# Memory attention of a hybrid decoder layer: score sums with the sequence pair innermost, the last head's queries spread by products, a score step moved ahead of the sums, the weights in two tiles

## The chip, the cores and the metric

The kernel runs on one core of a Trainium2 chip. The metric is the device time of one execution in microseconds (us): 939.5 before the change, the median of three runs (939.25, 939.5 and 940.07). A core has five engines with a queue of instructions each, which run side by side and wait for one another by semaphores: PE (TensorE, matrix products into PSUM; its weight loads are listed as PEld), DVE (VectorE), ACT (ScalarE), POOL (GpSimd) and SP (SyncE, which issues the DMAs here). Within one queue instructions start in the order in which they were built.

## The reference, cut to what matters

One layer of a decoder serves a prompt group (512 rows) and a sample group (8 sequences of 4 new rows) with the same weights: a mixer of mLSTM and differential attention, a cross-attention into 256 memory tokens, and a gated MLP with a short convolution. The change lies in the cross-attention alone:

```python
def mem_attend(h, mk, mv, w_mq, w_mo):
    B, T, _ = h.shape
    q = (h @ w_mq).reshape(B, T, MEM_HEADS, MEM_HEAD_DIM)
    s = jnp.einsum('bqhd,bkhd->bhqk', q.astype(jnp.float32), mk.astype(jnp.float32)) * (MEM_HEAD_DIM ** -0.5)
    p = jax.nn.softmax(s, axis=-1)
    o = jnp.einsum('bhqk,bkhd->bqhd', p, mv.astype(jnp.float32)).reshape(B, T, D_MODEL)
    return o.astype(h.dtype) @ w_mo
```

There are 4 heads of 256 dimensions. The prompt attends to keys and values computed from its own memory tokens (mk, mv); each sample sequence has its own cached K and V (`cache_mem_k`, `cache_mem_v`, 256 x 1024 values each).

## The kernel before, in words

All matrices are f32. For precision the large products take a value as a rounded "hi" part and the remainder as a "lo" part: `split` (L146, L147) has ACT cast the hi part and DVE subtract it. The products of the queries, `hqT` by `w_mq`, run in eight column blocks (L485); their evacuation `ev_q` leaves the prompt's queries as `qh` and `ql` and the 32 sample rows as `qs`.

**Prompt.** Eight steps, one for each head and half of the rows, pass through three stages: `ch_soft` (scores `sca`, 12 products, then maximum `cnm`, exponential and division into `cp`), `ch_turn` (four transposes `cpt` on PE, split into `pT`), and `ch_out` (for a whole head, 12 products `cpo`, split into `oT`). `pipe` issues them so that in turn t come the out of step t - 3, the turn of step t - 2 and the scores of step t; each `next(prompt)` issues one turn. The turns are the fill between the sample group's parts.

**Sample.** For 8 sequences x 4 rows x 4 heads, products are 32 columns wide, and four of them lie side by side in PE's 128 columns, one column group each. `mq_spread` copies each head's 32 sample queries to `qx` (heads 0 and 1) or `both` (heads 2 and 3), four groups of 32 partitions and four positions each, 16 small copies for each of heads 2 and 3, 32 for the others; zeros around them were set ahead. `mk_load` loads K images of two halves, `mk_turn` has DVE transpose them in blocks of 32. `mk_scores` (L1519) computes the scores `ssc` of a pair of sequences, first with heads 0 and 1 (e = 0), then with heads 2 and 3 (e = 1), and ACT copies them to `sc` (L1522). `mk_sum` (L1536) adds up the four column groups of the eight scores with 16 products `pS` against a selector, into one bank: sequence pair i goes to the 32 columns from 32 i. Then `mem_softmax`, which is scheduled with high priority: maximum from `pS` (L1553), `over_groups` (two block transposes, a reduction and a copy, L1540 to L1545), subtraction (L1554), exponential on ACT (L1555), sum, division (L1556, L1557), transposes `spt` on PE (L1566), and ACT's copies (L1569) to the weights `caz`, 128 x 2048, cleared by POOL (L1559). `mv_out` (L1587) multiplies them with the V images into `pso`. After the last head's `cpo`, the projection with `w_mo` begins (L411 to L413).

**What sets the order.** The code is written in the order shown; a scheduler places each instruction on its engine's queue by its readiness, with `burst` and `issue_after` holding a group of products together. Buffers come from pools: `S` (11 large tiles), `N` (5), `stage()` (6), and PSUM pools for `mmp` (5 banks) and `at` (3). A tile takes the slot of the pool's least recently used one, so which tile is asked for decides when a later load, such as `cr` (the 24 small loads of the convolution's state and weights, L1646 to L1648, in an N tile), finds room.

## Time and profile before

| | us |
|---|---|
| median of 3 runs | 939.5 |
| the profiled execution, on its own | 939.88 |
| its span, from the first to the last instruction | 938.1 |
| PE busy | 914.0 (97%) |
| DVE, ACT, POOL busy | 607.4 (65%), 377.8 (40%), 223.7 (24%) |
| mean granted TensorE clock | 0.996 |
| cross-attention, from the queries to the first product with w_mo | about 395 to 479 |

The table is of the one execution that the profiler took. A row of the timeline gives start, duration, engine, line, operation, output and inputs, a count, and in brackets how long the engine had been idle and what released it. Rows overlap a little, since the ends of pipelined instructions are modelled; where a cost is taken from rows, the distance from one start to the next counts. A product of plain f32 values is two PE instructions in the trace.

### The profile page before, as it was taken

How to read it: one execution, taken by the hardware profiler on the slowest of the kernel's cores; microseconds unless marked ns; L12 is line 12 of the kernel's file. 1: busy time of each engine (PE TensorE's matmuls, PEld its weight loads, DVE VectorE, ACT ScalarE, POOL GpSimd, SP SyncE). 2: the span in 40 equal slices, each digit the busy share in tenths (PEclk: the TensorE clock that was granted, in tenths of full speed). 3: DMA queues.
4: the chain of work that ended last, by engine and by line, in shares of the span. 5: the costliest groups of instructions: out<-in, count | busy, mean ns of one | idle time of the engine just before them, and what ended most of it. 6: DMA issues, size and time to landing. Idle time of an engine off the chain costs nothing.

```text
span 938.1 us, 17455 instructions
## 1 busy us (share of the span) xinstructions
PE 914.0 (97%) x6778; PEld 798.0 (85%) x6778; DVE 607.4 (65%) x1130; ACT 377.8 (40%) x728; POOL 223.7 (24%) x474
## 2 busy tenths in 40 slices
PE   7999999999999999999999999999999999999994
PEld 5899787879866778998777899889988998999974
DVE  5845144565887438686645778637757775776767
ACT  5745233344586447724434533322212222222232
POOL 6611000034442116570000553001100110110114
PEclk9999999999999999999999999999999999999998
DMA  8950023334780339967956632062054304413023
GB/s 286 311 180 11 1 90 138 90 103 161 243 296 8 136 117 298 310 201 243 312 189 172 198 115 69 26 180 69 27 135 135 92 5 120 128 48 90 24 94 117
DMA packets 120834, 130.59 MB, mean 139 GB/s; under 512 B 8599, under 2 KB 86264, under 8 KB 120752
## 3 DMA queue, kind: packets, MB, share of 16 engines
q1 hardware_dynamic: 114568, 125.96, 42.8%
q10 hardware_dynamic: 6184, 3.53, 1.3%
q8 instruction: 53, 0.87, 0.4%
q14 instruction: 29, 0.24, 0.1%
HBM read 112.54 MB, written 16.93 MB: 138 GB/s over the span
## 4 chain that ended last, share of the span: by engine, by line
PE 79%; DVE 8%; DMA 5%; ACT 3%; issue 3%; POOL 2%; SPq 0%; DVEq 0%; ACTq 0%; POOLq 0%
PE mm L485 31%; PE mm L411 6%; PE mm L412 6%; PE mm L413 6%; PE mm L472 4%; PE mm L1837 3%; PE mm L1841 3%; PE mm L1840 3%; PE sda L1256 2%; DVE xb L1165 2%; DMA wst<-in_cache_mem_k_dram 1%; PE mm L390 1%; PE cpo L1480 1%; DVE wslot L147 1%; PE oda L1284 1%
## 5 line engine op out<-in xcount | busy, mean ns | idle before, releaser
L485 PE MATMUL mm<-fT,wslot 128*128 128x256 f32 x1872 | 235.9, 288 | 0.0
L485 PEld LDWEIGHTS mm<-fT,wslot 128*128 128x128 f32 x1872 | 234.3, 188 | 1.8 <-issue 0.8
L146 ACT CAST wslot<-wst 128x1024 fp32r<-128x1024 f32 x125 | 130.7, 1050 | 261.0 <-issue 72.5
L147 DVE TENSOR_TENSOR wslot<-wst,wslot 128x1024 fp32r<-128x1024 f32 x125 | 154.3, 1238 | 81.7 <-ACT wslot L146 81.1
L1837 PE MATMUL mm<-wslot,act 128*128 128x512 f32 (+1 forms) x180 | 69.3, 387 | 0.0
L1840 PE MATMUL mm<-wslot,act 128*128 128x512 f32 (+1 forms) x172 | 67.0, 391 | 0.0
L1841 PE MATMUL mm<-wslot,act 128*128 128x512 f32 (+1 forms) x172 | 66.8, 392 | 0.0
L1739 POOL COPY cvo<-u 128x2 f32<-128x2 f32 x43 | 10.4, 243 | 217.1 <-DVE u L1737 217.1
L411 PE MATMUL mm<-wslot,hT 128*128 128x512 f32 x128 | 51.3, 402 | 0.0
L413 PE MATMUL mm<-wslot,hT 128*128 128x512 f32 x128 | 51.0, 399 | 0.0
L485 PE MATMUL mm<-hT,wslot 128*128 128x256 f32 (+1 forms) x384 | 50.9, 289 | 0.0
L412 PE MATMUL mm<-wslot,hT 128*128 128x512 f32 x128 | 50.8, 397 | 0.0
L1734 DVE TENSOR_TENSOR u<-mm,rsb 128x256 f32<-128x256 f32 x43 | 18.1, 423 | 48.9 <-PE mm L485 48.8
L485 PEld LDWEIGHTS mm<-hT,wslot 128*128 128x128 f32 x384 | 49.2, 188 | 0.5 <-issue 0.2
L1837 PEld LDWEIGHTS mm<-wslot,act 128*128 128x128 f32 x180 | 34.3, 191 | 8.0 <-issue 0.4
L1841 PEld LDWEIGHTS mm<-wslot,act 128*128 128x128 f32 x172 | 32.3, 188 | 6.9 <-issue 0.4
L1840 PEld LDWEIGHTS mm<-wslot,act 128*128 128x128 f32 x172 | 32.3, 188 | 6.9
L1751 ACT ACTIVATE c<-c 128x560 f32<-128x560 f32 x21 | 14.1, 672 | 56.8 <-DVE c L1745 56.7
L1745 DVE SCALAR_TENSOR_TENSOR c<-u,cvT,c 128x560 f32<-128x560 f32 x43 | 34.3, 798 | 0.9
L1744 DVE SCALAR_TENSOR_TENSOR c<-u,cvT,c 128x560 f32<-128x560 f32 x43 | 34.1, 793 | 0.2
L1852 DVE TENSOR_TENSOR yp<-mm,yp 128x512 f32<-128x512 f32 (+1 forms) x41 | 27.1, 672 | 5.1 <-PE mm L1841 5.1
L413 PEld LDWEIGHTS mm<-wslot,hT 128*128 128x128 f32 x128 | 24.1, 188 | 5.0
(493 smaller groups left out, 1858.0 us busy)
## 6 DMA issues: line engine op xcount, KB each, us to landing
wst<-in_w_up_dram SPq DMA_DIRECT2D x42, 512.0 KB
wst<-in_w_in_dram SPq DMA_DIRECT2D x28, 512.0 KB
wst<-in_w_down_dram SPq DMA_DIRECT2D x20, 512.0 KB
kvt<-in_cache_mem_k_dram SPq DMA_DIRECT2D x10, 512.0 KB
kvt<-in_cache_mem_v_dram SPq DMA_DIRECT2D x10, 512.0 KB
wst<-in_w_mk_dram SPq DMA_DIRECT2D x8, 512.0 KB
xb<-in_x_prompt_dram SPq DMA_DIRECT2D x8, 512.0 KB
wst<-in_cache_dk_dram SPq DMA_DIRECT2D x16, 256.0 KB
```

Of the source, the lines that this page charges most:

```text
L146: nc.scalar.copy(out=hi, in_=src)
L147: (eng or nc.vector).tensor_tensor(out=lo, in0=src, in1=f32(hi), op=SUB)
L411: mm(ps[b], lhsT=xt.hi(k, c0, c0 + n), rhs=s[:, 0, kk, :], start=(k == 0), stop=False)
L412: mm(ps[b], lhsT=xt.hi(k, c0, c0 + n), rhs=s[:, 1, kk, :], start=False, stop=False)
L413: return mm(ps[b], lhsT=xt.lo(k, c0, c0 + n), rhs=s[:, 0, kk, :], start=False, stop=(k == nk - 1))
L472: done[0] = mm(ps, lhsT=s[:, l, k, :], rhs=x(k, c0, c1), start=(k == 0 and l == 0 and x == xt.hi), stop=(k == 7 and x == xt.lo))
L485: mm(ps[i], lhsT=s[:, l, k, :], rhs=x(k, c0, c1), start=(k == 0 and j == 0), stop=(k == 7 and j == 2))
L1744: STT(out=c, in0=u[:, 1:EXT - 1], scalar=w[1], in1=c, op0=MUL, op1=ADD)
L1745: STT(out=c, in0=u[:, 0:EXT - 2], scalar=w[0], in1=c, op0=MUL, op1=ADD)
L1837: mm(ps, lhsT=t[:, 0, c0:c0 + P], rhs=s[:, 0, i % 2, cs], start=st, stop=False)
L1840: mm(ps, lhsT=t[:, 0, c0:c0 + P], rhs=s[:, 1, i % 2, cs], start=False, stop=False)
L1841: return mm(ps, lhsT=t[:, 1, c0:c0 + P], rhs=s[:, 0, i % 2, cs], start=False, stop=en)
```

## The change

1. **Queries of the last head.** The 16 copies of head 3 are replaced: four products against `four` (four copies of the identity's slices, made once by POOL) spread `qs` to all four partition groups in PSUM (`qsp`), and four copies, two on DVE and two on ACT, bring them to `both`. `qh` is evacuated ahead of the spread.
2. **Sums.** `mk_sum` runs over the sequence pair i innermost, so successive products go to different column groups; before, i was outermost and four in a row went to one.
3. **A score step ahead.** `pipe` is replaced by `steps`. At t = 6 it issues the scores of step 6 first and yields, which lets them be issued ahead of `mk_sum`; out and turn follow in the next call.
4. **Weights in two tiles.** `caz` is two N tiles of 128 x 1024, cleared after the fifth sequence's scores, instead of one S tile of 128 x 2048.

```diff
+    four = T2([P, 4, P], "four")
+    nc.gpsimd.tensor_copy(out=four.rearrange("p j (g m) -> p j g m", g=4), in_=view(ident, 0, [(NS, 4), (0, 4), (1, NS)]))
 
     def mq_spread(h):
 
+        if h == 3:
+            ps = at("qsp")[:, :256].rearrange("p (c j r) -> p c j r", c=2, j=4)
+            for j in range(4):
+                mm(ps[:, :, j], lhsT=four[:, j], rhs=qs[:, 6:8], start=True, stop=True)
+            for g in range(4):
+                o = slice(NS * g, NS * g + NS)
+                copy = nc.scalar.copy if g % 2 else VCP
+                copy(out=both[o, :, :, :, 1, g, :].rearrange("p c j n t -> p c (j n) t"),
+                     in_=ps[o].rearrange("p c j (n t) -> p c (j n) t", t=TS))
+            return
         for g in range(4):
-            copy = nc.scalar.copy if h == 3 and g > 1 else nc.gpsimd.tensor_copy
+            copy = nc.gpsimd.tensor_copy
...
                 nc.scalar.mul(out=qs[:, m, :], in_=ps[:, n:n + NS], mul=1.0 / 16.0)
-                if m % 2 == 1:
+                if m % 2 == 1 and m < 7:
                     mq_spread(m // 2)
             nc.scalar.mul(out=q, in_=ps[:, :n], mul=1.0 / 16.0)
+            if i == 1 and m == 7:
+                mq_spread(3)
...
-        for i in range(NB // 2):
-            for h in range(2):
-                for e in range(2):
+        for h in range(2):
+            for e in range(2):
+                for i in range(NB // 2):
...
-        az = S([P, 2, H, NB * NS], F32, "caz")
-        nc.gpsimd.memset(az, 0.0)
...
-            nc.scalar.copy(out=view(az, c * 1024, [(256, H), (36, NB), (1, TS)]),
+            nc.scalar.copy(out=view(az[c], 0, [(256, H), (36, NB), (1, TS)]),
...
-    prompt = pipe(8, ch_soft, lambda i: None, ch_turn, ch_out)
+    def steps():
+        for t in range(11):
+            soft, rest = step(t)
+            if t == 6:
+                soft()
+                yield
+                rest()
+            else:
+                rest()
+                soft()
+            yield
+
+    prompt = steps()
...
+        if b == 4:
+            for _ in range(2):
+                az.append(N("caz").rearrange("p (h n) -> p h n", h=H))
+                nc.gpsimd.memset(az[-1], 0.0)
+    next(prompt)
     mk_sum(t)
     with tc.high_priority():
-        az = mem_softmax()
+        mem_softmax()
```

`step(t)` returns two functions: `soft` calls `ch_soft(t)`, `rest` calls `ch_out(t - 3)` and `ch_turn(t - 2)`.

How the built order differs at three places. On PE, where the last queries meet the first score pair; before, from the first products of pair (0,1) on:

```order
L1519 MATMUL ssc<-wst,qx 32x2x32 x34
L1468 MATMUL cpt<-cpk,cp 128x128 x4
L1519 MATMUL ssc<-wst,qx 32x2x32 x30
L1450 MATMUL sca<-mkT,qh 128x256 x2
L1450 MATMUL sca<-mkT,ql 128x256
```

and after:

```order
L1533 MATMUL ssc<-wst,qx 32x2x32 x16
L1415 MATMUL qsp<-qs,four 128x2x32 x4
L1533 MATMUL ssc<-wst,qx 32x2x32 x16
L1482 MATMUL cpt<-cpk,cp 128x128 x4
L1464 MATMUL sca<-mkT,qh 128x256 x2
L1464 MATMUL sca<-mkT,ql 128x256
```

The spreading products stand between the two sequences' first halves, and the scores of step 3 (sca) now come ahead of the pair's second half, the 32 products with `both`. On DVE the copies of that spread, in the changed kernel:

```order
L1467 TENSOR_REDUCE cnm<-sca 128x2
L1516 STREAM_TRANSPOSE kvt<-kvt 128x1024
L147 TENSOR_TENSOR pT<-cpt,pT 128x256
L1419 COPY qx<-qsp 32x64x4
L1516 STREAM_TRANSPOSE kvt<-kvt 128x1024
L1471 RECIPROCAL csu<-csu 128x2
L147 TENSOR_TENSOR pT<-cpt,pT 128x256
L1419 COPY qx<-qsp 32x64x4
```

The two transposes are those of K image 7. The second place is that of the sums. On PE, before:

```order
L1519 MATMUL ssc<-kvt,qx 32x128 x32
L1536 MATMUL pS<-sc,cpk 32x2x64 x12
L1480 MATMUL cpo<-pT,mvN 128x512 x2
L1536 MATMUL pS<-sc,cpk 32x2x64
L1480 MATMUL cpo<-pT,mvN 128x512 x5
L1536 MATMUL pS<-sc,cpk 32x2x64 x3
L1480 MATMUL cpo<-pT,mvN 128x512 x5
L1468 MATMUL cpt<-cpk,cp 128x128 x4
```

and after, where the 12 sca products of step 6, of which the last two rows are shown, stand between the scores and the sums:

```order
L1464 MATMUL sca<-mkT,qh 128x256 x2
L1464 MATMUL sca<-mkT,ql 128x256
L1550 MATMUL pS<-sc,cpk 32x2x64 x3
L1494 MATMUL cpo<-pT,mvN 128x512 x2
L1550 MATMUL pS<-sc,cpk 32x2x64 x13
L1494 MATMUL cpo<-pT,mvN 128x512 x10
L1482 MATMUL cpt<-cpk,cp 128x128 x8
```

On DVE behind the sums, before (oT is the lo part of out(3), one for each `cpo`):

```order
L1459 TENSOR_SCALAR cp<-cp,csu 128x256 x2
L1553 TENSOR_REDUCE spc<-pS 128x4
L147 TENSOR_TENSOR oT_5337<-cpo,oT_5336 128x512
L1540 STREAM_TRANSPOSE spc<-spc 128x32
L1541 TENSOR_REDUCE spc<-spc 128x8
L1544 COPY spc<-spc 128x32
L1545 STREAM_TRANSPOSE spc<-spc 128x32
L147 TENSOR_TENSOR oT_5337<-cpo,oT_5336 128x512
L1554 TENSOR_TENSOR spc<-pS,spc 128x256
```

and after:

```order
L1473 TENSOR_SCALAR cp<-cp,csu 128x256 x2
L147 TENSOR_TENSOR oT_5332<-cpo,oT_5331 128x512 x2
L1567 TENSOR_REDUCE spc<-pS 128x4
L147 TENSOR_TENSOR pT<-cpt,pT 128x256 x2
L1554 STREAM_TRANSPOSE spc<-spc 128x32
L1467 TENSOR_REDUCE cnm<-sca 128x2
L147 TENSOR_TENSOR pT<-cpt,pT 128x256
L1555 TENSOR_REDUCE spc<-spc 128x8
L147 TENSOR_TENSOR pT<-cpt,pT 128x256
L1558 COPY spc<-spc 128x32
L1559 STREAM_TRANSPOSE spc<-spc 128x32
```

Both lo parts stand ahead of the maximum now. The third place is SP's queue of DMAs. Before, the `cr` loads stand between K and V images:

```order
L1498 DMA kvt<-in_cache_mem_k_dram 128x1024 x8
L1646 DMA cr<-in_state_conv_dram 16x896
L1647 DMA cr<-in_w_dw_dram 3x896
L1648 DMA cr<-in_b_dw_dram 1x896
L1646 DMA cr<-in_state_conv_dram 16x896
L1647 DMA cr<-in_w_dw_dram 3x896
L1648 DMA cr<-in_b_dw_dram 1x896
L1498 DMA kvt<-in_cache_mem_k_dram 128x1024 x2
```

and after they stand behind nearly all V images:

```order
L1512 DMA wst<-in_cache_mem_k_dram 128x1024 x6
L1512 DMA kvt<-in_cache_mem_k_dram 128x1024 x10
L1588 DMA wst<-in_cache_mem_v_dram 128x1024 x6
L1588 DMA kvt<-in_cache_mem_v_dram 128x1024 x8
L1689 DMA cr<-in_state_conv_dram 16x896
L1690 DMA cr<-in_w_dw_dram 3x896
```

More of the change, by code (lines that the diff above doesn't have):

```diff
@@ L1568, in mem_softmax @@
         for c in range(2):
-            nc.scalar.copy(out=view(az, c * 1024, [(256, H), (36, NB), (1, TS)]),
+            nc.scalar.copy(out=view(az[c], 0, [(256, H), (36, NB), (1, TS)]),
                            in_=pT[:, c * P:c * P + P].rearrange("p (h b t) -> p h b t", h=H, b=NB))
-        return [az[:, 0], az[:, 1]]
     def mv_load(b):
@@ L1588, in mv_out, with step, soft, rest @@
                            rhs=vts[b][c][:, 256 * h:256 * h + 256], start=((b, c) == VORD[0]), stop=((b, c) == VORD[-1])).ins
-    prompt = pipe(8, ch_soft, lambda i: None, ch_turn, ch_out)
+    az = []
+    def step(t):
+        def soft():
+            if t < 8:
+                ch_soft(t)
+        def rest():
+            if 0 <= t - 3 < 8:
+                ch_out(t - 3)
+            if 0 <= t - 2 < 8:
+                ch_turn(t - 2)
+        return soft, rest
+    def steps():
[10 more added lines that the diff above has]
+    prompt = steps()
     pS = at("pS")[:, :256]
```

## The prediction

> **What bounds the kernel now.** I read the page first, then the stretches, PE's waits, and PE's timeline in the stretch that the diff touches.
>
> ```profile
> PE 79%; DVE 8%; DMA 5%; ACT 3%; issue 3%; POOL 2%; SPq 0%; DVEq 0%; ACTq 0%; POOLq 0%
> 430.00:480.00 50.00, 46.46 (x745) 37.38 (x744) 32.61 (x73) 25.17 (x76) 3.78 (x10) 1.00 0.89 305
> 480.00:545.00 65.00, 65.00 (x400) 53.23 (x399) 41.39 (x73) 29.03 (x58) 17.57 (x28) 1.00 0.58 167
> 545.00:900.00 355.00, 354.69 (x2538) 331.45 (x2541) 248.29 (x431) 94.80 (x114) 46.32 (x190) 1.00 0.28 79
> ```
>
> The chain that ended last is PE for 79%. The rows below it are stretches: length, busy time of PE, PEld, DVE, ACT, POOL, then granted clock, DMA share, GB/s. From 480 to 900 us PE never rests, at full clock: what the change does before 479, where the output projection starts, arrives at the end of the kernel undiminished. In 430 to 480 PE idles 3.54 us of 50, and PE's waits name where:
>
> ```profile
> PE ssc L1519 <- DVE ql L1434: 1.5, 1, 1.5
> PE pso L1587 <- ACT caz L1569: 1.0, 1, 1.0
> PE spt L1566 <- DVE spc L1557: 0.8, 1, 0.8
> ```
>
> So nearly everything here costs PE time; the sum is: where does PE stand at the start of the first L411 product, now 479.04. I walk the built order of the changed kernel with durations from these rows, in three stretches, against the profiled execution's 939.88 us.
>
> **First stretch, queries and the first score pairs.** Columns: start, duration, engine, line, operation.
>
> ```profile
> 433.24 0.65 PE L1519 MATMUL ssc<-wst,qx 128*32 128x64 f32 x32
> 435.37 0.75 PE L1519 MATMUL ssc<-wst,qx 128*32 128x64 f32 x36 [1.48 <-DVE ql L1434]
> 436.06 0.66 PE L1468 MATMUL cpt<-cpk,cp 128*128 128x128 f32 x4
> 436.64 1.09 PE L1519 MATMUL ssc<-wst,qx 128*32 128x64 f32 x60
> 437.69 0.50 PE L1450 MATMUL sca<-mkT,qh 128*128 128x256 f32 x2
> ...
> 441.21 3.28 PE L1480 MATMUL cpo<-pT,mvN 128*128 128x512 f32 x12
> ```
>
> ```profile
> 433.24 1.25 DVE L1502 STREAM_TRANSPOSE kvt<-kvt 128x1024 f32<-128x1024 f32 x1 [1.10 <-DMA kvt<-in_cache_mem_k_dram]
> ...
> 435.90 0.68 DVE L1453 TENSOR_REDUCE cnm<-sca 128x2 f32<-128x512 f32 x1
> ...
> 439.24 1.25 DVE L1502 STREAM_TRANSPOSE kvt<-kvt 128x1024 f32<-128x1024 f32 x1 [1.21 <-DMA kvt<-in_cache_mem_k_dram]
> ```
>
> Removed: 16 small copies of the last head's queries, 8 each on POOL and ACT.
>
> ```profile
> 432.86 2.05 ACT L1415 COPY qx<-qs 32x64 f32<-32x64 f32 x8
> 437.07 0.47 ACT L1456 ACTIVATE cp<-sca,cnm 128x256 f32<-128x256 f32 x1
> ```
>
> ACT's end at 434.91, and PE needs them only at the second half of pair (0,1), about 435.4: nothing waited long. In their place come four products (8 PE instructions, L1415) and two copies each on DVE and ACT. The products have no row; nearest is the cpt group at 436.06, 4 full-width instructions set between score groups, 0.58 us to the next start. I take **+0.45** (eight narrower ones; at 0.03 each, as in a score group, 0.24; at 0.58 the upper end).
>
> The order then pulls the t = 3 scores (sca) ahead of the second half of pair (0,1). Now that sca starts at 437.69, 0.15 after the exponential that empties its bank (437.07 + 0.47); 60 score instructions, 1.09 us, covered the wait. In the changed kernel PE gets there about 436.2 and the exponential still hangs on the reduction at 435.90: **+1.3** of waiting (0.8 if the reduction comes 0.5 earlier; 1.5).
>
> The second half then needs the DVE and ACT copies. DVE's second copy is queued behind both transposes of K image 7. From the reduction: 435.6 + 0.65 (reduction) + 1.2 (transpose) + 0.35 (pT) + 0.33 (copy) + 1.2 + 0.1 (reciprocal) + 0.35 (pT) + 0.33 gives 440.1. The copy has no row on DVE; nearest is the pT subtraction of as many elements a partition, 0.41 long and 0.33 from start to start (463.42, below). PE has finished sca about 438.9 and a few more score products by 439.2: **+0.9** (0 if K's transposes come earlier by as much; 1.1). ACT's second copy stands behind a cast and ends no later.
>
> Against that, the 1.48 wait for ql shrinks. DVE reaches ql behind the K transpose at 433.24, which waited 1.10 for its DMA. SP's queue explains it:
>
> ```profile
> 424.06 3.60 SPq L1498 DMA_DIRECT2D kvt<-in_cache_mem_k_dram  x4
> 428.37 0.33 SPq L1646 DMA_DIRECT2D cr<-in_state_conv_dram  x1
> ...
> 431.48 2.11 SPq L1498 DMA_DIRECT2D kvt<-in_cache_mem_k_dram  x2
> ```
>
> With the weights in two N tiles the 24 small cr loads get a later slot and all move behind V loads; K image 7 is issued before 431.48 and lands before DVE asks. I take **-1.2** (0 if K lands as late as now). Sum of the stretch: 0.45 + 1.3 + 0.9 - 1.2 = **+1.5** (-0.2 to 3.2 with all terms at their ends); the first cpo group starts at 442.7 instead of 441.21.
>
> **Second stretch, to the sums.**
>
> ```profile
> 450.18 1.96 PE L1519 MATMUL ssc<-kvt,qx 128*32 128x128 f32 x64
> 452.39 2.00 PE L1536 MATMUL pS<-sc,cpk 128*32 128x128 f32 x24 [0.26 <-issue]
> 454.32 0.74 PE L1480 MATMUL cpo<-pT,mvN 128*128 128x512 f32 x2
> 454.99 0.41 PE L1536 MATMUL pS<-sc,cpk 128*32 128x128 f32 x2
> 455.32 1.43 PE L1480 MATMUL cpo<-pT,mvN 128*128 128x512 f32 x5
> 456.68 0.84 PE L1536 MATMUL pS<-sc,cpk 128*32 128x128 f32 x6
> 457.45 1.41 PE L1480 MATMUL cpo<-pT,mvN 128*128 128x512 f32 x5
> 458.70 0.60 PE L1468 MATMUL cpt<-cpk,cp 128*128 128x128 f32 x4
> 459.06 0.48 PE L1450 MATMUL sca<-mkT,qh 128*128 128x256 f32 x2
> ...
> 460.56 0.60 PE L1468 MATMUL cpt<-cpk,cp 128*128 128x128 f32 x4
> ...
> 462.44 2.95 PE L1480 MATMUL cpo<-pT,mvN 128*128 128x512 f32 x12
> ```
>
> The cpo group at 441.21 took 0.33 longer than the one at 462.44: it waited inside for pT, which is ready when it starts 1.5 later. So the last scores end at 452.13 + 1.5 - 0.35 = 453.3 (452.13 is 450.18 + 1.96). Then the score step that was moved ahead, 1.6 us (459.06 to 460.56 is 1.5, and a return to full width): 454.9.
>
> The sums: 32 instructions in 2.00, 0.41 and 0.84 us, 1.93 / 24 = 0.080 each by starts in the long group. The score group above puts four column groups in turn, at equal width, and needs 1.96 / 64 = 0.031 each. With the pair innermost the sums have that pattern: 32 x 0.031 = 0.98 against 3.03 by starts, and two pieces instead of three spare one change of width: from 452.39 to 458.70 are 6.31, **4.35** after (6.3 if the sums gain nothing). Sums and cpo end at 459.25.
>
> [...]
>
> **Third stretch, the sample softmax on DVE.**
>
> ```profile
> 457.63 0.42 DVE L1553 TENSOR_REDUCE spc<-pS 128x4 f32<-128x256 f32 x1 [3.15 <-PE pS L1536]
> ...
> 458.90 0.59 ACT L146 CAST oT<-cpo 128x512 fp32r<-128x512 f32 x1 [1.76 <-PE cpo L1480]
> 459.52 0.69 DVE L147 TENSOR_TENSOR oT<-cpo,oT 128x512 fp32r<-128x512 f32 x1
> ...
> 463.42 0.41 DVE L147 TENSOR_TENSOR pT<-cpt,pT 128x256 fp32r<-128x256 f32 x1
> 463.75 0.61 DVE L1459 TENSOR_SCALAR cp<-cp,csu 128x256 f32<-128x256 f32 x2
> ...
> 466.19 0.41 DVE L1557 TENSOR_TENSOR spc<-spc 128x256 f32<-128x256 f32 x1
> 466.66 0.76 PE L1566 MATMUL spt<-cpk,spc 128*32 128x32 f32 x64 [0.84 <-DVE spc L1557]
> 468.38 2.80 PE L1587 MATMUL pso<-wst,caz 128*32 128x256 f32 x48 [0.96 <-ACT caz L1569]
> ```
>
> This is the term that decides. Before, the maximum (L1553) started right behind the sums, ahead of both lo parts of out(3). In the changed order it stands behind both, so it waits for the last cpo product, its cast and its subtraction, as the ACT and DVE rows at 458.90 and 459.52 show (0.2 after PE's end, 0.62, 0.69): 459.25 + 0.2 + 0.62 + 0.65 = 460.7. What PE gained in the sums thus buys the chain nothing. From the maximum to the product DVE needs 8.97 us now (457.63 to 466.60), with 15 foreign instructions between. In the changed order there are 12: one oT (0.69), one cnm (0.68), one reciprocal (0.2) and two cp (0.61) fewer, two pT (0.41 each) more, 1.4 us of durations or 1.2 as they overlap: **7.8** (8.97 if the queue does not close up; 4.0 for its own steps alone, that is 7.8 less what the 12 cost, below). The product ends at 468.5 and spt starts at 468.55, against 466.66.
>
> PE meanwhile has the old fill from 458.70 to 465.82 (7.12 us) less the moved score step (1.5): 459.25 + 5.6 = 464.85. It waits **3.7** instead of 0.84. The 0.96 ahead of pso stays: the copies to the two weight tiles are the same two. Tile clears on POOL go to about 439, beside PE; I cost them at nothing, up to 0.5 if a cp in the first stretch is held. The `four` copy on POOL stands ahead of a 2048-wide clear; nothing waits for it. V loads gain from cr's move, but pso did not wait for V. So L411 starts 468.55 - 466.66 = 1.9 later; with 0.1 for what the DVE copies push back, **+2.0**: 939.88 + 2.0 = 941.9. That execution lies 0.4 above the median of 939.5, so in medians I say **941.5**.
>
> [...]
>
> **The rivals.**
>
> *K loads no earlier.* If K image 7's second half still lands at 439.2 (DMAs run at a share of 0.89 in this stretch, so a place ahead in the queue need not be an earlier landing), DVE's second copy moves to 441.2, and the ql wait keeps up to 0.8: +0.9 to +1.7 more, **942.8**. For it the DMA share; against it that the gap between 427.66 and 431.48 in SP's queue is filled by six cr loads, the first of them quoted.
>
> *The first stretch costs nothing.* If the copies are ready before PE asks and the exponential comes early, +0.2 instead of +1.5 reaches the chain: **940.2**, no change to measure. Against it DVE's fixed queue with two 1.25 transposes.
>
> *The softmax chain is short (the other side).* Place: DVE between maximum and product. If the foreign work finds its inputs late enough to be out of the way, or the built queue drains without stalls, every us below 7.8 is a us at the end; at 5.9 the kernel is level, at 4.0 PE's fill decides and spt starts at 464.85: -1.8, **938.0** to 939.0. For it: 0.84 was all that PE waited so far. Against it: the instructions stand in DVE's queue in that order, and the 12 sum to 5.3 us (six pT at 0.41, two oT at 0.69, the cp pair 0.61, cnm 0.68, a reciprocal 0.2), some 3.8 once the overlap from start to start is taken off.
>
> *The sums don't overlap.* If four column groups in turn gain nothing there, 6.3 instead of 4.35 us; the chain starts 1.95 later: **943.5**. Against it the score row.
>
> **How the numbers follow.** A measurement of this kernel can tell some 0.2%, 1.9 us, from no change. Chances: forecast 0.50 (own range 940.8 to 942.5), K loads no earlier 0.15, first stretch free 0.15, short chain 0.13, no overlap 0.07. The forecast lies near the 0.2% bound of 941.4: I count 0.30 of its 0.50 as slower, the rest as same. Slower 0.30 + 0.15 + 0.07 = 0.52; same 0.20 + 0.15 = 0.35; faster 0.13. The range runs from 939.4 (short chain mostly left out) to 943.5 (which takes in the two late cases).
>
> **What would show it.** In the changed kernel's profile: the sums in two pieces near 0.03 us an instruction; a PE wait of about 3.7 us at spt for the last product of the softmax, with the maximum starting after the second lo part of out(3), near 460.7; waits of about 1 us each at sca for an exponential and at ssc for qx near 436 and 439; no cr load between K images; the first L411 product at 481.0. I am wrong if the spt wait is under 2 us, if the sums keep 0.08 an instruction, or if anything after L411 changes by over 0.5 us.

## The result, and the profile after

| | before | after |
|---|---|---|
| median | 939.26 us (5 runs, 939.22 to 940.07) | 944.22 us (5 runs, 942.95 to 944.29) |
| ratio to before, 95% interval | | 1.0047 [1.0033, 1.0061] |
| profiled execution, its span | 939.88, 938.10 us | 942.95, 941.18 us |
| mean granted TensorE clock | 0.996 | 0.993 |

The changed kernel is slower by 0.47% by the ratio (0.33 to 0.61); the two medians lie 5.0 us apart. The forecast of 941.5 us (939.4 to 943.5) had the sign, and less than half of the size.

The same stretches as before, of the changed kernel (length; busy time of PE, PEld, DVE, ACT, POOL; granted clock; DMA share; GB/s):

```profile
430.00:480.00 50.00, 44.28 (x738) 34.73 (x736) 29.49 (x73) 22.32 (x68) 1.10 (x2) 0.93 0.73 260
480.00:545.00 65.00, 65.00 (x386) 52.50 (x383) 41.19 (x72) 28.72 (x56) 15.15 (x25) 1.00 0.62 186
545.00:900.00 355.00, 355.00 (x2547) 332.83 (x2546) 248.61 (x433) 97.05 (x118) 48.87 (x193) 1.00 0.28 82
```

From 480 us on all is as it was: PE without a pause, at full clock. In 430 to 480 PE idles 5.72 us instead of 3.54, and the clock reads 0.93: that is new, and no term of the forecast has it. PE's waits from 395 to 485 us, then PE's timeline there:

```profile
PE spt L1578 <- DVE spc L1571: 3.4, 1, 3.4
PE ssc L1533 <- ACT qx L1419: 0.9, 1, 0.9
PE sca L1464 <- ACT cp L1470: 0.7, 1, 0.7
PE mm L485 <- DVE ql L1448: 0.7, 1, 0.7
PE pso L1598 <- ACT caz L1581: 0.6, 1, 0.6
```

```profile
434.04 1.10 PE L1415 MATMUL qsp<-qs,four 128*128 128x64 f32 x8
437.01 0.51 PE L1464 MATMUL sca<-mkT,qh 128*128 128x256 f32 x2 [0.69 <-ACT cp L1470]
440.19 1.10 PE L1533 MATMUL ssc<-wst,qx 128*32 128x64 f32 x64 [0.90 <-ACT qx L1419]
442.83 3.05 PE L1494 MATMUL cpo<-pT,mvN 128*128 128x512 f32 x12
455.09 0.42 PE L1550 MATMUL pS<-sc,cpk 128*32 128x128 f32 x6
456.10 1.06 PE L1550 MATMUL pS<-sc,cpk 128*32 128x128 f32 x26
...
464.05 1.17 PE L1494 MATMUL cpo<-pT,mvN 128*128 128x512 f32 x4
468.66 1.08 PE L1578 MATMUL spt<-cpk,spc 128*32 128x32 f32 x64 [3.45 <-DVE spc L1571]
470.35 4.71 PE L1598 MATMUL pso<-wst,caz 128*32 128x256 f32 x48 [0.60 <-ACT caz L1581]
482.95 0.63 PE L411 MATMUL mm<-wslot,oT 128*128 128x512 f32 x2
```

Up to spt the marks of the forecast hold to some 0.1 us: cpo at 442.83 (442.7 foretold), the sums in two pieces, spt at 468.66 (468.55) after a wait of 3.45 (3.7). Behind it the same 64 products of spt take 1.08 us instead of 0.76, and the 48 of pso 4.71 instead of 2.80. The stretches of one us around it show why (the column ahead of the last two is the clock; the last row is from the end of the kernel):

```profile
467.00:468.00 1.00, 0.00 (x0) 0.00 (x0) 0.90 (x5) 0.00 (x0) 0.00 (x0) 0.73 0.01 4
468.00:469.00 1.00, 0.34 (x25) 0.37 (x29) 0.48 (x2) 0.00 (x0) 0.00 (x0) 0.50 0.26 68
474.00:475.00 1.00, 1.00 (x17) 0.31 (x9) 0.00 (x0) 0.00 (x0) 0.00 (x0) 0.86 0.94 365
935.00:936.00 1.00, 0.00 (x0) 0.00 (x0) 0.25 (x2) 0.24 (x2) 0.43 (x1) 0.54 0.00 0
```

In PE's wait the granted clock falls to 0.50. With 1.00 on one side and 0.50 on the other, a mean of 0.73 over one us is 0.54 us at 0.50, so it fell at 467.46; 0.86 is 0.28 us, so it came back at 474.28, 6.82 us later. The products in between take longer: spt's 1.08 is 1.4 times its old 0.76, and 3.93 of pso's 4.71 us lie there; half of them and the 0.78 behind are some 2.75, near its old 2.80.

The changed kernel was traced five times (this one, and e13, e16, e17, e18 below: 942.95, 942.44, 943.75, 944.19 and 942.17 us, mean 943.1). The column of before is its one trace. Each stretch runs from the first product of one group to that of the next; in us:

| stretch | before | after, five traces | mean change | forecast |
|---|---|---|---|---|
| start to hqT by w_mq (L485) | 403.89 | 403.72 to 404.40 | +0.1 | 0 |
| to the first score ssc | 29.35 | 29.74 to 30.57 | +0.7 | 0 |
| to the first cpo group | 7.97 | 9.21 to 9.40 | +1.4 | +1.5 |
| to the sums pS | 11.18 | 12.23 to 12.26 | +1.1 | +1.0 |
| to spt | 14.27 | 13.55 to 13.58 | -0.7 | -0.6 |
| to the first product with w_mo (L411) | 12.38 | 13.18 to 14.56 | +1.5 | 0 |
| to the end | 459.06 | 458.21 to 458.33 | -0.8 | +0.1 |

Two stretches at which the forecast put nothing carry the miss of the traces: the queries, and what follows spt.

### The profile page after: what moved, and what is told of

It reads as the page before. It is cut to its first block, busy times and chain, and to the rows that moved or that the text cites. A ratio compares the mean times of both kernels' runs of the same rounds, so it can differ in the third digit from the quotient of the medians.

```text
span 941.2 us, 17479 instructions
## 1 busy us (share of the span) xinstructions
PE 917.5 (97%) x6786; PEld 799.8 (85%) x6786; DVE 609.1 (65%) x1132; ACT 377.0 (40%) x722; POOL 221.7 (24%) x468
## 4 chain that ended last, share of the span: by engine, by line
PE 87%; DVE 6%; DMA 4%; ACT 1%; issue 1%; POOL 0%; DVEq 0%; ACTq 0%; SPq 0%; POOLq 0%
PE mm L485 32%; PE mm L472 8%; PE mm L412 7%; PE mm L411 7%; PE mm L413 7%; PE mm L1880 3%; PE mm L1884 3%; PE mm L1883 3%; PE sda L1256 2%; PE mm L390 2%; PE tp L332 1%; PE oda L1284 1%; DMA mem_d<-ht 1%; PE cpo L1494 1%; PE pso L1598 1%
## 5 line engine op out<-in xcount | busy, mean ns | idle before, releaser
L485 PE MATMUL mm<-fT,wslot 128*128 128x256 f32 x1872 | 235.9, 288 | 0.0
L485 PEld LDWEIGHTS mm<-fT,wslot 128*128 128x128 f32 x1872 | 234.3, 188 | 1.8 <-issue 0.8
L411 PE MATMUL mm<-wslot,hT 128*128 128x512 f32 x128 | 51.3, 402 | 0.0
L485 PE MATMUL mm<-hT,wslot 128*128 128x256 f32 (+1 forms) x384 | 51.0, 289 | 0.0
L485 PEld LDWEIGHTS mm<-hT,wslot 128*128 128x128 f32 x384 | 49.2, 188 | 0.5 <-issue 0.2
L1787 DVE SCALAR_TENSOR_TENSOR c<-u,cvT,c 128x560 f32<-128x560 f32 x43 | 34.1, 793 | 0.2
```

Source lines behind the costliest of these rows:

```text
L411: mm(ps[b], lhsT=xt.hi(k, c0, c0 + n), rhs=s[:, 0, kk, :], start=(k == 0), stop=False)
L485: mm(ps[i], lhsT=s[:, l, k, :], rhs=x(k, c0, c1), start=(k == 0 and j == 0), stop=(k == 7 and j == 2))
L1787: STT(out=c, in0=u[:, 1:EXT - 1], scalar=w[1], in1=c, op0=MUL, op1=ADD)
```

## The experiments

All kernels, by what they take of the change; "own" means that the softmax maximum and its helpers have memory of their own.

| kernel | queries | sums | step | weights | maximum in | median, us | ratio [95%] |
|---|---|---|---|---|---|---|---|
| after | products | new | ahead | two | pool | 944.22 | 1.0047 [1.0033, 1.0061] |
| e13, after again | products | new | ahead | two | pool | 944.19 | 1.0058 [1.0042, 1.0074] |
| e1, three filler products | products | new | ahead | two | pool | 944.04 | 1.0054 [1.0041, 1.0067] |
| e2, maximum first | products | new | ahead | two | pool | 944.25 | 1.0060 [1.0042, 1.0078] |
| e6, `four` on ACT | products | new | ahead | two | pool | 942.26 | 1.0033 [1.0021, 1.0046] |
| e10 | products | new | old | two | pool | 944.06 | 1.0043 [1.0028, 1.0058] |
| e5 | products | new | ahead | two | own | 943.83 | 1.0035 [1.0021, 1.0048] |
| e14, `four` on ACT | products | new | ahead | two | own | 941.92 | 1.0026 [1.0015, 1.0037] |
| e3 | 16 copies | new | ahead | two | pool | 941.13 | 1.0019 [1.0011, 1.0028] |
| e12, three filler products | 16 copies | new | ahead | two | pool | 940.09 | 0.9997 [0.9985, 1.0009] |
| e8 | 16 copies | new | ahead | two | own | 937.41 | **0.9973 [0.9963, 0.9983]** |
| e9 | 16 copies | new | ahead | one | own | 939.31 | 0.9994 [0.9984, 1.0004] |
| e15 | 16 copies | new | old | two | pool | 938.28 | 0.9990 [0.9979, 1.0002] |
| e11 | 16 copies | new | old | one | pool | 939.96 | 0.9996 [0.9985, 1.0007] |
| e7, before and an unused `four` | 16 copies | old | old | one | pool | 940.44 | 1.0006 [0.9997, 1.0015] |
| e4, before and 12 self-copies | 16 copies | old | old | one | pool | 945.40 | 1.0065 [1.0052, 1.0078] |

The medians of before in the batches run from 938.96 to 940.27, so kernels of different batches are compared by ratio; 0.001 is 0.94 us. The fillers, the self-copies and the unused `four` are work added, and nothing reads what they make.

### The wait and the clock: e1, e4, e12

The first theory, the clock's: PE's pause makes the clock fall, and the fall costs 1.9 us behind it. e1 breaks the pause with products between exponential and spt; nothing else in the order moves.

```diff
+        pT = at("spt")
+        for _ in range(3):
+            mm(pT[:, 256:512], lhsT=ident, rhs=a, start=True, stop=True)
```

> The changed kernel with three extra products in PE's wait for the softmax: they read the exponentials (ready about 465.0) and write an unused half of spt's bank, so they add nothing to the chain and the order of all other instructions stays. Theory C (clock): the granted clock fell to 0.50 at about 468 because PE had been idle 3.45 us, and that halved spt and the first pso group (1.08 and 4.71 us instead of 0.76 and 2.80). Then spt still starts at 468.6 +- 0.3, but at clock 1.00, the first pso group takes 2.8, the first L411 product starts at 481.0 +- 0.3 instead of 482.95, and the median is 941 to 942. Theory V (the pso group waited for V images or for the two weight tiles): the pso group keeps 4.7 us, L411 stays at 483, the median at 944.

e1, PE's timeline from the fillers on:

```profile
468.02 1.56 PE L1572 MATMUL spt<-spc,cpk 128*128 128x256 f32 x6
471.58 0.76 PE L1580 MATMUL spt<-cpk,spc 128*32 128x32 f32 x64 [2.00 <-DVE spc L1574]
472.92 2.80 PE L1600 MATMUL pso<-wst,caz 128*32 128x256 f32 x48 [0.58 <-ACT caz L1583]
```

The pause is 2.00, the clock stays at 1.00, spt and pso take their old 0.76 and 2.80: from spt to L411 12.03 us against 14.29. The median did not follow (944.04): in this trace the query stretch is 2.4 us longer, 32.14 against 29.74, by waits of PE for `ql` (2.8 in all). In the trace the clock is confirmed: with it at 1.00 the products behind the wait take their old time. The median, foretold as 941 to 942, does not show the gain; a second thing moves between executions.

e4 goes the other way: the kernel before, its chain made longer by 12 copies of a softmax tile onto itself.

```diff
+        for _ in range(12):
+            VCP(out=a, in_=a)
```

> The kernel before with twelve copies of the softmax weights onto themselves ahead of spt, so that PE's wait of 0.84 us becomes 0.84 + d; d is read from the trace (0.2 to 0.35 a copy, so 2.4 to 4.2). Theory C: if the wait passes some 3 us, the granted clock falls to 0.50 for 4 to 8 us behind it, and the time rises by d + 2 to 3 us. Theory V: it rises by d alone, and the clock stays at 1.00.

```profile
471.98 1.08 PE L1568 MATMUL spt<-cpk,spc 128*32 128x32 f32 x64 [5.77 <-DVE spc L1559]
```

With none of the change in it, a longer wait brings the same half clock (spt 1.08). It lay from 469.24 to 476.07, 2.7 us of it in the wait, so behind spt it costs 13.53 - 12.38 = 1.2 us here, less than the 2 to 3 expected. The 3 us of the expectation was the author's estimate, from the one wait of 3.45; no run shows it as a bound.

e12 adds e1's fillers to e3, the changed kernel with the 16 copies.

> The e3 kernel (changed kernel with the 16 copies) with three filler products on PE between the exponential and spt, whose result nothing uses; the rest of the order is that of e3. Theory (PE's unbroken idle of 3.4 us makes the granted clock fall to half for some us): the wait is split, the clock stays at 1.00, spt takes 0.76 and the first pso group 2.8 us, and it is 1.3 to 1.9 us faster than e3's 941.1: 939.2 to 939.9. Rival (the clock falls for another reason, or its fall costs nothing in the end): 941.1 or more, since the fillers add work.

```profile
467.72 0.76 PE L1566 MATMUL spt<-cpk,spc 128*32 128x32 f32 x64 [2.01 <-DVE spc L1560]
469.01 4.28 PE L1586 MATMUL pso<-wst,caz 128*32 128x256 f32 x48 [0.52 <-ACT caz L1569]
```

Half met: the median is 940.09, the ratio 0.0022 (2.1 us) better than e3's, but the clock fell in the traced execution all the same, after a pause of only 2.01, and pso took 4.28. It stayed at 0.50 for 3.41 us, against 6.83 in e3. A pause of 2.0 us thus goes without a fall in e1 and with one in e12; the last section sets the two side by side.

### What makes the maximum late: e2, e5

The forecast put the maximum (460.7, measured 460.94) behind out(3)'s lo parts by DVE's order. e2 puts those lo parts behind the maximum.

```diff
+            with tc.issue_after(first[0]) if first and h == 1 else nullcontext():
                 put(oT, h // 2, j, j + 1, 0, SEQ, po.unsqueeze(1))
...
+        first.append(VRED(out=mx[:, 0:H], in_=v2(pS, 64), axis=AX.X, op=MAX).ins)
```

> The changed kernel, with the two lo parts of out(3) put behind the maximum of the sums in DVE's queue. If the late start of the maximum (460.9, behind both lo parts) is what makes PE's wait of 3.45 us: the maximum starts at 457.2 to 457.5, the chain holds two oT more (1.3 us) and ends near 466.2, PE waits about 1.0, the clock stays at 1.00, the first L411 product starts at 478.5 to 479.2, the median is 939 to 940. Rival (the chain ends late for what is queued behind the maximum, not for its start): spt starts at 467.5 or later, the median is above 940.5.

DVE in the changed kernel, then in e2; POOL in the changed kernel, then in the kernel before:

```profile
460.33 0.69 DVE L147 TENSOR_TENSOR oT<-cpo,oT 128x512 fp32r<-128x512 f32 x1 [0.69 <-ACT oT L146]
460.94 0.41 DVE L1567 TENSOR_REDUCE spc<-pS 128x4 f32<-128x256 f32 x1
```

```profile
460.96 0.42 DVE L1570 TENSOR_REDUCE spc<-pS 128x4 f32<-128x256 f32 x1 [2.50 <-POOL spc L1568]
```

```profile
460.17 0.15 POOL L1565 MEMSET spc<- 128x64 f32 x1 [20.57 <-PE cpt L1482]
```

```profile
448.94 0.15 POOL L1551 MEMSET spc<- 128x64 f32 x1 [14.41 <-PE cpt L1468]
```

In the changed kernel the maximum starts right behind the second lo part, as foretold. Moved ahead of both in e2, it starts no earlier (457.2 to 457.5 was expected), and DVE stands idle ahead of it for 2.50 us: it waits for POOL's clear of its own tile, which in e2 starts at 460.78. `spc` shares three buffers with the probabilities `cp`. The step put ahead takes one more of them, so `spc` gets that of step 4, free only after its transposes `cpt`, at 460.17 instead of 448.94. So two bounds lie close together. In the changed kernel the clear at 460.17 would have let the maximum start at about 460.35 (0.18 behind it, as in e2), 0.6 us ahead of the lo parts' end; the forecast saw only the later one. e5 gives `spc` memory of its own:

```diff
-        z = Z("spc")
-        nc.gpsimd.memset(z[:, 256:320], 1.0)
+        a, z = cst.tile([P, 256], F32, name="spa", tag="warm"), cst.tile([P, 104], F32, name="spc")
+        nc.gpsimd.memset(z[:, 0:64], 1.0)
```

> The changed kernel with the sample softmax's work tile (spc) in memory of its own instead of the pool of three that it shares with the prompt's cp. Theory S (slot): the score step put ahead takes the third cp tile, so spc gets the slot of step 4's cp, its clearing on POOL waits for that step's transposes (460.17), and the maximum for the clearing, whatever DVE's order. With a tile of its own the maximum starts at 457.2 to 457.6, PE waits less than 1 us at spt, the clock stays at 1.00, the first L411 product starts 4.5 to 5.5 earlier than 482.95, the median is 938.7 to 940. Theory Q (queue: what stands behind the maximum on DVE makes the chain long): the maximum is early, but spt still waits over 2 us, the median is above 941.

e5, from DVE, PE, SP and ACT:

```profile
458.23 0.42 DVE L1567 TENSOR_REDUCE spc<-pS 128x4 f32<-128x256 f32 x1 [1.31 <-PE pS L1550]
466.13 0.76 PE L1578 MATMUL spt<-cpk,spa 128*32 128x32 f32 x64
480.21 0.74 PE L411 MATMUL mm<-wslot,oT 128*128 128x512 f32 x2 [1.83 <-ACT wslot L146]
473.63 3.31 SPq L231 DMA_DIRECT2D wst<-in_w_mo_dram  x6
479.11 1.04 ACT L146 CAST wslot<-wst 128x1024 fp32r<-128x1024 f32 x1 [6.88 <-DMA wst<-in_w_mo_dram]
```

With a buffer at hand the maximum is also placed ahead of both lo parts (459.97 and 461.37 in e5). It starts 2.7 us earlier, and PE waits for spt no more; spt to L411 is 14.08 with a new wait in it. For the next bound is bare: `w_mo`, whose load SP issues at 473.63 (469.07 in the kernel before), arrives after PE is there. PE waits 1.8 and then 0.5 us, the clock falls at 480.81, and L411 to the next block's products takes 83.78 us instead of 80.18. The ratio moves by 0.0012 alone, within what the intervals leave open; the expected 938.7 to 940 was missed.

### The copy to `four`: e6, e7

The forecast had it on POOL with "nothing waits for it". But with it the scheduler puts two transposes of K images together on DVE, ahead of a `ql`. DVE in the changed kernel, then in e6, where ACT makes the copy:

```profile
398.65 2.45 DVE L1516 STREAM_TRANSPOSE wst<-wst 128x1024 f32<-128x1024 f32 x2 [4.67 <-DMA wst<-in_cache_mem_k_dram]
...
402.13 0.41 DVE L1448 SCALAR_TENSOR_TENSOR ql<-mm,qh 128x256 fp32r<-128x256 f32 x1
```

```profile
399.73 1.25 DVE L1516 STREAM_TRANSPOSE wst<-wst 128x1024 f32<-128x1024 f32 x1 [5.08 <-DMA wst<-in_cache_mem_k_dram]
...
402.00 0.41 DVE L1448 SCALAR_TENSOR_TENSOR ql<-mm,qh 128x256 fp32r<-128x256 f32 x1
402.34 1.23 DVE L1516 STREAM_TRANSPOSE wst<-wst 128x1024 f32<-128x1024 f32 x1
```

```diff
-    nc.gpsimd.tensor_copy(out=four...
+    nc.scalar.copy(out=four...
```

> The changed kernel with the four identity copies made by ACT instead of POOL; nothing else is edited, but in the built order DVE's transposes of K images 0 and 1 then alternate with the ql parts again, as before the change, instead of two transposes ahead of a ql. Theory O (order): each transpose waits for a K load, so two ahead of a ql make PE wait for the bank that this ql empties: 0.7 us in the changed kernel's profile, 1.4 and 2.8 in two executions of its variants, 0.3 before. Then PE's wait for ql around 416 is 0.3 to 0.7 again, and the median falls by 0.5 to 1.5 us to 942.7 to 943.7. Rival (loads simply land later in these executions): 944.

e7 adds the copy on POOL, unused, to the kernel before.

> The kernel before with the four identity copies made by POOL and not used by anything; the built order then shows DVE's two transposes ahead of a ql. Theory O: PE's wait for ql around 416 rises from 0.3 to 0.7 or more, the median rises by 0.5 to 1.5 us, to 939.9 to 940.9. Rival: 939.4.

e7's DVE has the doubled order, so the copy alone makes it. Its price is small: e6 is 0.0014 (1.3 us) better than the changed kernel with intervals that overlap, e7 0.0006 worse than before with an interval that takes in 1. By traces, hqT to the first score is 29.74 to 32.14 us, mean 30.4, in the ten with the doubled order (the five of the changed kernel, e1, e2, e5, e7, e10), and 29.16 to 30.65, mean 29.7, in the ten with the old one. The waits for `ql` hang on when a K load lands and occur in both orders (e12 1.4 us). I take the 0.7 us between the means as its size; the ranges overlap, so it is a mean over landings and not a price of each execution.

### Products or copies: e3, e8, e14

e3 is the changed kernel with the 16 copies of head 3's queries back.

```diff
-    four = T2([P, 4, P], "four")
...
-        if h == 3:
-            ps = at("qsp")[:, :256].rearrange("p (c j r) -> p c j r", c=2, j=4)
...
+            copy = nc.scalar.copy if h == 3 and g > 1 else nc.gpsimd.tensor_copy
```

> The changed kernel with the last head's queries spread by the 16 copies of before, all else changed. If the spread by products costs 1.5 us in the first stretch (products, a wait at sca, a wait at ssc): the first cpo group starts at 441.2 or, with the K image earlier, down to 440, all behind it 1.5 to 2.7 earlier, spt's wait still 3.4 us with the clock at 0.50 behind it, the median 941.5 to 942.8. If the spread costs nothing that reaches the end: 944.

e8 is e3 and e5 together: copies, and the maximum in memory of its own.

> The changed kernel with spc in memory of its own and the last head's queries spread by the 16 copies of before: the sums with the pair innermost, the score step ahead and the weights in two tiles are kept. If the losses add up as read: what the tile brings (4.5 to 5 us) and what the copies bring (3.1 us, 944.2 less 941.1) give 935.8 to 937.2, 2 to 3.5 us faster than before. If the two losses overlap: 938 to 939.

```profile
461.86 0.76 PE L1564 MATMUL spt<-cpk,spa 128*32 128x32 f32 x64
463.29 2.80 PE L1584 MATMUL pso<-wst,caz 128*32 128x256 f32 x48 [0.67 <-ACT caz L1567]
473.95 0.63 PE L411 MATMUL mm<-wslot,oT 128*128 128x512 f32 x2
478.27 0.44 PE L1663 MATMUL ost<-cpk,oS 128*128 128x128 f32 x2 [1.15 <-ACT oS L1660]
```

e3 (1.0019) shows that the products cost more than the copies they replace: ssc to the first cpo group takes 6.91 us in e3 and 7.12 in e8, against 9.2 to 9.5 wherever the products stand. The 1.4 against the kernel before (7.97) were foretold; but the 7.97 held the wait for `ql` that the two weight tiles take away, so by themselves the products cost some 2.3.

e8 beats both kernels, by 0.27% and 0.74%. Its trace, the fastest of its eleven executions, has no wait at spt, the clock at 1.00 up to PE's last product, and L411 at 473.95, 5.1 us ahead of the kernel before; 1.15 us are given back ahead of `ost`.

SP in e5, then in e8:

```profile
441.70 3.72 SPq L1588 DMA_DIRECT2D wst<-in_cache_mem_v_dram  x6
```

```profile
435.33 4.37 SPq L1574 DMA_DIRECT2D wst<-in_cache_mem_v_dram  x6
466.43 3.60 SPq L231 DMA_DIRECT2D wst<-in_w_mo_dram  x6
```

e8 has the 24 `cr` loads ahead of `w_mo` too, and no wait for it. What differs begins earlier: the first V loads wait for a score product `ssc` to set their tiles free, 8.1 us at the longest in e5 and 4.1 in e8; with the products the second half of the scores of pair (0,1) comes later. In all eleven traces with the products the first V load goes out 7.05 to 7.35 us behind the first ssc, in the nine with the copies 2.8 to 4.1; `w_mo`, queued behind, follows at 38.5 to 39.7 against 33.2 to 35.5 (41.1 in e4, with its longer chain). So the late `w_mo` goes with the products, not with the 24 loads; no run parts the two costs of the products.

e14 leaves the products and mends the other two: own memory, and `four` on ACT.

> The e5 kernel (the changed kernel, softmax maximum in memory of its own) with the copy to the spreading weights, four, on ACT instead of POOL. Theory (four on POOL costs about 1.1 us in the query stretch, the slot costs the spt wait): no spt wait of over 0.5 us, no ql wait of over 0.5 us, spt near 465.3; what is left over e8 is the products' 1.5 us and the late w_mo (PE waits at the first product with it): 941 to 942.5. Rival (the products themselves cost more than the rows show): 943.5 or more.

Met: spt at 465.95 without a wait, 0.3 for `ql`, median 941.92. What is left over e8, 0.0053 or 5.0 us, was foretold in kind: ssc to cpo 9.51 (2.4 more), and waits of 2.5 and 0.5 us for `w_mo` with a fall of the clock (its mean from 480 to 545 us is 0.95, as in e5, against 1.00 in e8; L411 to the next block 83.80, 2.5 more than in e8).

### Each of the other parts: e9, e10, e11, e15

e9 is e8 with the weights in one tile again.

> The e8 kernel (16 copies of the last head's queries, the softmax maximum in memory of its own), with the weights caz again as one S tile of 128 x 2048 made and cleared after the sums. This returns the 24 small cr loads to their place between the K loads and takes them away from ahead of the w_mo load. Against e8's 937.4: if the two-tile weights help by the earlier K image and hurt by the later w_mo, and both are about 1 us, 936.9 to 938.0; if only the K side counts, the ql wait returns and it is slower, about 938.3; if only the w_mo side counts, the projection's weights arrive about 3 us earlier and it is faster, about 936.2 (first product with w_mo to the next block 80.1 us instead of 81.3).

e9, PE and SP:

```profile
436.11 0.75 PE L1519 MATMUL ssc<-wst,qx 128*32 128x64 f32 x36 [1.58 <-DVE ql L1434]
471.96 0.64 PE L1587 MATMUL pso<-kvt,caz 128*32 128x256 f32 x8 [1.18 <-DMA kvt<-in_cache_mem_v_dram]
467.09 5.49 SPq L231 DMA_DIRECT2D wst<-in_w_mo_dram  x6
```

The waits for `ql` return (1.6 ahead of ssc), and new ones for V loads come (1.8 in two). The median is 939.31, beyond the 938.3 that the K side alone was to cost: against e8 the two tiles gain 0.0021, 2.0 us. `w_mo` goes out at 467.09, no earlier than in e8 (466.43; behind the first ssc 33.2 against 34.1 us), so the price that the expectation put on its delay is hardly there.

e11 is the kernel before with the new order of the sums alone; e15 has the sums and the two tiles; e10 is the changed kernel with the old `pipe`.

```diff
-        for i in range(NB // 2):
-            for h in range(2):
-                for e in range(2):
+        for h in range(2):
+            for e in range(2):
+                for i in range(NB // 2):
```

> The kernel before with one edit: the sums with the sequence pair innermost. Theory: the sums take 1.9 us less on PE (0.038 us an instruction instead of 0.08), but the softmax chain then hangs behind the output's lo parts, so most of it is given back as a longer wait ahead of spt (1.5 to 3 us instead of 0.84): 938.5 to 939.2. Rival A (the gain reaches the end): 937.6. Rival B (the clock falls in the wait): 940 to 941.

> The e3 kernel (16 copies of the last head's queries) with the old pipe: new order of the sums and weights in two tiles alone. Theory (the two tiles give about 2 us by the earlier K image, the sums give their 1.9 us back at spt): spt wait about 2 us as in e11, ql waits under 0.6, 937.5 to 938.8, close to e8 (937.4); then the step ahead is worth nothing by itself and costs 3 us where its buffer is taken from the softmax. Rival (the step ahead is needed): 940 or more.

> The changed kernel with the old pipe: the score step is not put ahead of the sums. Queries by products, the new order of the sums and the weights in two tiles stay. Theory (the step takes the softmax's buffer and the fill from under the chain): the maximum starts about 458.6 behind both lo parts instead of 460.94, spt at about 467.3 with a PE wait of about 1.5 us, the clock stays at 1.00, the first product with w_mo at 479.7 to 480.2 instead of 482.95: 941 to 942. Rival (the step is not what costs; the shortened sums alone bare the chain): spt waits 3 us or more, the clock falls, 944.

PE in e11, then in e10:

```profile
464.31 0.76 PE L1566 MATMUL spt<-cpk,spc 128*32 128x32 f32 x64 [2.09 <-DVE spc L1557]
465.69 4.48 PE L1587 MATMUL pso<-wst,caz 128*32 128x256 f32 x48 [0.63 <-ACT caz L1569]
```

```profile
469.26 0.91 PE L1578 MATMUL spt<-cpk,spc 128*32 128x32 f32 x64 [2.15 <-DVE spc L1571]
470.75 3.92 PE L1598 MATMUL pso<-wst,caz 128*32 128x256 f32 x48 [0.58 <-ACT caz L1581]
```

e11: from the sums to spt it is 13.84 us instead of 14.27, and without the wait at spt, which grows from 0.84 to 2.09, 11.75 instead of 13.43: the sums gain 1.7, the wait takes 1.25 of it, the clock falls for 3.41 us (pso 4.48), and the median is that of before (0.9996). e15 came out as foretold, 938.28, with the same wait. Beside e11 it adds the two tiles alone, and is 0.0006 (0.6 us) better with intervals that overlap; so the two tiles gain somewhere between 0.6 and 2.0 us. Beside e3 (1.0019) and e8 (0.9973) e15 says what the step is worth: with its buffer taken from the softmax it costs 0.0029 (2.7 us), with a buffer for both it gains 0.0017 (1.6 us; here too the intervals overlap). e10 missed its expectation: the wait is 2.15, not 1.5, the clock falls for 3.41 us, and the median stays at 944.06. From ssc to L411 it is 47.11 against the changed kernel's 49.49, as the theory wants; in this trace the query stretch (31.01) and L411 to the next block (81.52 against 79.76, with 1.1 of waiting ahead of `ost`) take that back. So beside the products the step's price does not show in the median.

### Other executions: e13, e16, e17, e18

The changed kernel with no edit, to see what differs between its executions.

> The changed kernel as it is, in another set of executions, to see what differs between its executions. Theory (the half clock follows windows of 3.41 us whose phase is another in each execution, and the wait for ql hangs on a K load's landing): the ratio to before is again 1.004 to 1.006; the maximum again waits for POOL's clear of its buffer and the PE wait ahead of spt is again 3.4 to 3.5 us; but the clock falls at another time after the wait's start, for 3.41 or 6.83 us, and the ql wait is between 0.7 and 2.8 us. Rival (the profiled execution stands for all): the clock falls 2.2 us after the wait's start for 6.83 us, and the ql wait is 0.7.

The clock in e13, in stretches of one us:

```profile
469.00:470.00 1.00, 0.54 (x63) 0.43 (x49) 0.00 (x0) 0.36 (x2) 0.00 (x0) 0.98 0.30 72
473.00:474.00 1.00, 1.00 (x20) 0.54 (x16) 0.00 (x0) 0.00 (x0) 0.00 (x0) 0.82 0.85 238
934.00:935.00 1.00, 0.00 (x0) 0.00 (x0) 0.76 (x4) 0.51 (x2) 0.00 (x0) 0.58 0.00 0
```

The wait at spt is 3.44 as before, but here the clock fell at 469.96, behind spt, and came back at 473.36: 3.40 us instead of 6.82.

> The changed kernel as it is, one more execution with a trace. Theory: hqT to ssc between 29.7 and 32.1 us by the ql wait, spt to the first product with w_mo between 13.5 and 14.3 us by how much of the half clock falls on products; in an execution of 944 us or more the ql waits come to 1.5 us or more, or the half clock lies whole on products. Rival: such an execution differs after the first product with w_mo (projection and later), by over 0.8 us.

> As e16_third, one more execution of the changed kernel: what its stretches give beside the first two (942.95 and 942.44).

> As e16_third, one more execution of the changed kernel, with the same two theories on where a longer one is longer.

The execution of 944.19 (e17) differs from that of 942.17 (e18) by 0.5 ahead of the queries, 0.4 in the query stretch and 1.4 from spt to L411 (clock at 0.50 for 6.83 against 3.41 us); after L411 the five agree within 0.12. Its `ql` wait is 1.2, less than the 1.5 I had set, but the half clock lies on products, as the theory has it (over a wider range, 13.18 to 14.56, than I gave); the rival falls. The one run of the kernel before beside these three took 943.01, above nearly all its others, so no ratio is drawn from them.

## Why the prediction was wrong, point by point

- *First stretch, +1.5.* Right in sum: 9.34 against 7.97 is +1.4. Of its terms, the spreading products took 1.04 from start to start (434.04 to 435.08; +0.45 taken), the wait at sca 0.69 (+1.3 taken), that at ssc 0.90 (+0.9), and the 1.48 for `ql` went whole (-1.2 taken); the three costs sum to 2.63, 2.65 taken. That the sum holds is luck: two terms are off by 0.6, one each way. The rival that the K loads come no earlier falls.
- *Second stretch, 4.35 us for sums and cpo.* Right: 455.09 to 459.51 is 4.42, and an instruction of the long piece takes (457.09 - 456.10) / 26 = 0.038 us. It owes something to luck as well: the forecast's own terms give 6.31 - (3.03 - 0.98) = 4.26, less still with a change of width spared, and 0.038 in place of 0.031 adds 0.2. The price of a change of width, which the forecast spares here and adds as 0.1 to the step put ahead, no run shows by itself; in the kernel before the four cpt take 0.58 us to the next start between score groups (436.06) and 0.36 ahead of sca (458.70). That the sums do not overlap falls.
- *Third stretch, maximum at 460.7, chain 7.8, spt at 468.55.* Right to 0.3 in each (460.94, 7.6, 468.66), with half of the cause for the first: the lo parts end last, but the buffer from the shared pool binds 0.6 us ahead of them, and with a buffer of its own the maximum is not placed behind them at all (e2, e5). The short chain falls: from the maximum to the product it is 7.5 us in e5 and e8 too. There it starts earlier, and in e8 PE's fill decides.
- *"So L411 starts 468.55 - 466.66 = 1.9 later".* **This is the step that failed.** It moves the block behind spt as it was, at full clock. In five traces the block from spt to L411 is 13.18 to 14.56 us long instead of 12.38, +1.5 in the mean; with the wait ahead of pso shorter by 0.36, the half clock itself costs about 1.8. e1 at full clock took 12.03, e4 shows the same fall without the change.
- *"The `four` copy on POOL ...; nothing waits for it".* The second one: no product waits for the copy, but DVE's order in the query stretch is another with it (e6, e7). About +0.7 in the traces.
- *"V loads gain from cr's move".* They don't: with the products the first goes out at 440.67 instead of 437.10. Here nothing waits for it; in e5 and e14 PE waits for `w_mo` behind it.
- *After L411, +0.1.* The traces give -0.8, of which about 0.4 is that the traced execution of before was itself long there (378.88 us from the next block on; 378.2 to 378.5 in all others). Two kernels that leave this part as it was, e7 and e4, took 458.08 and 458.38 in their traces against 458.21 to 458.33, so a change behind L411 is not shown.
- *The median.* Worked against its traced execution, the forecast was 941.9; the five traces have a mean of 943.1. I took 0.4 off for the median, as the kernel before would want it; the changed kernel's median, 944.2, lies 1.1 above its traces' mean instead. What the untraced executions do there stays open; the traces allow the place of the half clock and the `ql` wait, and show no more. That the half clock's price reaches the median is borne out by e12 against e3 (2.1 us, intervals apart; in the traces a fall half as long), but not by e1 (944.04).

By its parts, from the ratios: the two tiles gain 0.6 to 2.0 us. The sums gain 1.7 to 1.9 us on PE and nothing at the end while the softmax chain is bare. The step, beside the copies, gains 1.6 us with a buffer for the maximum and costs 2.7 without. The products for the queries cost 2.6 us (e3 to after) to 5.8 (e8 to e5).

## What to carry to other kernels

Where a wait of PE grows to some 2 us (the clock fell with 1.83 in e5 and 2.01 in e12, and stayed with 2.00 in e1), price the products behind it at 0.50 for 3.4 or 6.8 us, as these traces have it, and take more than one trace: the fall came 2.25 us after the start of the wait in the first trace and 4.61 in e13. Where a step is moved ahead of a critical chain, list the buffers that it takes from that chain's pools, not only its instructions in the queues. When one bound is taken away, look at once for the next, and for what sets its loads' tiles free: here scores that came later held the V loads back and `w_mo` behind them, which ate what the buffer had given. Before blaming what stands ahead in a queue, look at a run with the same queue and no wait.

## What the runs showed of the hardware

The granted clock reads 1.00 or 0.50 in these traces, and a mean between the two where a stretch holds a change. It fell during or after every wait at spt of 2.01 us or more: 2.01 in e12, 2.09 in e11, 2.15 in e10 and e15, 3.44 or 3.45 in the five traces of the changed kernel and in e2, e3 and e6, 5.77 in e4. It stayed at 1.00 around the 2.00 of e1 and the 0.84 of the kernel before and of e7. The half clock lasted 6.82 or 6.83 us in the first trace, e2, e3, e4, e5 and e17, and 3.40 to 3.42 in e6, e10 to e13, e15, e16 and e18.

Where it falls differs from one execution to the next: at 467.46 in the first trace, ahead of spt (468.66), and at 469.96 in e13, behind it (468.79). After PE's last product it fell again, at 935.08 in the first trace (the stretch 935 to 936 at 0.54) and at 934.16 in e13. The distances are 467.62 us, 137 times 3.413, and 464.20, 136 times 3.413.

The length of one pause does not decide: in e5 the clock fell at 480.81, between waits of 1.83 and 0.52 for `w_mo`, and in e1 it stayed at 1.00 with waits of 2.00 and 0.58. Nor does the work of PE in a few us: the three from 470 in e1 hold 0.00, 0.42 and 0.42 us of products, at 1.00; the three from 466 in e12 hold 0.00, 0.28 and 0.49, and the clock fell at 468.64. What parts the two is not shown.

Products that go round four column groups took 0.038 us each in the sums (26 in 0.99 us by starts), against 0.080 with four in a row to one group (24 in 1.93, in the kernel before): a gain of 2.1 times, where the scores' 0.031 (64 in 1.96) had let expect 2.6.
